# LayerNorm's beta and the attention mask, added by accumulating DMAs instead of GpSimd instructions

## The chip, the cores and the metric

One Trainium2 chip, one of its cores. The metric is the device time of one execution in microseconds (us), from runs on the chip. The engines are TensorE (PE in the profile; PEld is its weight load), VectorE (DVE), ScalarE (ACT), GpSimd (POOL) and SyncE (SP). DMA transfers are issued from the queues of SP, ACT and POOL and share 16 DMA engines.

## What is computed

A trunk of two layers on 256 tokens of 2048 channels, float32. Layer 0 mixes tokens by a bidirectional gated linear attention, layer 1 by a neighbourhood attention of 16 heads on a 4 x 64 grid of tokens; after each mixer comes a gated feed-forward part with a convolution of width 3. Every sub-layer ends in a residual sum and a LayerNorm, four in all:

```python
x = _layer_norm(DEEPNORM_ALPHA * x + m, ln_mix_g[i], ln_mix_b[i])
f = _conv_ffn(x, ffn_w_up[i], ffn_conv_w[i], ffn_conv_b[i], ffn_w_down[i])
x = _layer_norm(DEEPNORM_ALPHA * x + f, ln_ffn_g[i], ln_ffn_b[i])
# _layer_norm: xc * rsqrt(var + eps) * g + b
# attention:   softmax(q k^T + bias), bias = NEG_INF outside the window of 16 columns
```

## The kernel before, in words

All weights (some 405 units of 1 MB, 128 partitions x 2048 floats) are streamed once from HBM. `unit_plan` is the order in which TensorE takes them. SP's queue loads each unit into one of three `raw` buffers (L127). The unit is then split into a rounded high part and a rest: ACT casts `hi` (L131), DVE subtracts to get `lo` (L132), each in four pieces of 128x512, into one of four pairs of buffers (`NS = 4`). A product is the sum of three float32r products, high x high, high x low and low x high (L190). A unit's buffers are free again when TensorE is through with it, and a `raw` buffer when its last `lo` has been made. The same pair of instructions splits every activation that is multiplied; for the output of a LayerNorm it goes from the tile `ln_f` into `xT`.

What is not a large product (gates, attention scores, LayerNorm) stands in a queue `side`; `later` puts a piece in, and `tick`, called between the matrix products, takes it out. Each engine executes its own list in order.

A sub-layer ends in `residual_out`: four blocks of 512 columns for two tiles of 128 tokens (t = 0, 1). The evacuation adds the product to the residual `x_sb` (L360, L362) and takes statistics (L366). The last block runs tile by tile (`apart`), so that the LayerNorm of tile 0 runs beside the products of tile 1. Three of the four LayerNorms are `ln_mid`:

- `head`: DVE aggregates (L282), POOL makes 1/sqrt(var + eps) in two small instructions (L274 `rs_m`, L275 `ln_rs`), DVE normalizes the four blocks of `x_sb` in place (L293).
- `turn`, four times: TensorE transposes four 128x128 pieces (L299), ACT and DVE multiply by gamma and add beta (L307, L309) into `ln_f`, and `emit_split` makes `xT` from it, which the next sub-layer multiplies.
- `resid`: POOL multiplies `x_sb` by gamma (L315) and adds beta (L316), block by block, for the residual that the next sub-layer's first block will read. `gb` holds gamma and beta, repeated on all partitions, 1 MB each (`load_gb`, L344, on POOL's queue).

The last LayerNorm (`ln_last`) writes the output and also uses POOL for one block per tile.

In the attention, each head loads its bias table `bt` (L701, POOL's queue, two buffers), POOL adds the mask to it (L702), and DVE adds `bt` to the scores (L724) when the head's queries and keys are done. In the feed-forward part POOL makes the first product of the convolution (L642) for each of 84 blocks of channels per layer.

Of the kernel before, what the change touches and what calls it, by code (L numbers as in the profile page):

```python
# [10 lines left out]
F32 = mybir.dt.float32  # L11
# [3 lines left out]
ALU = mybir.AluOpType  # L15
AX = mybir.AxisListType

P = 128
D = 2048
# [28 lines left out]
def unit_plan():  # L48
    """The 1 MB weight units in the order in which the tensor engine takes them."""
    plan = []  # L50
    for h in range(HG):
        plan += [("ws", "gla_in", h * 2 + c) for c in range(2)]
        plan += [("ws", "gla_in", 8 + h * 2 + c) for c in range(2)]
        if h == 0:
            plan += [("lr",)]
        plan += [("as", "gla_in", 4 + h, u) for u in range(4)]
        plan += [("as", "gla_in", 8 + h, u) for u in range(4)]
    plan += [("as", "gla_out", nb, u) for nb in range(4) for u in range(4)]
    for layer in range(DEPTH):
        if layer == 1:  # L60
            for g in range(4):
                plan += [("as", "na_in", 8 + g, u) for u in range(4)]
                for h in range(4 * g, 4 * g + 4):
                    plan += [("ws", "na_in", h), ("ws", "na_in", 16 + h)]
            plan += [("as", "na_out", nb, u) for nb in range(4) for u in range(4)]
        for c0, n in THIRDS:
            if c0 == 0:
                plan += [("pairs", f"up{layer}", u) for u in range(4)]
            for c in range(c0 + (2 if c0 == 0 else 0), c0 + n):
                plan += [("ws", f"up{layer}", c), ("ws", f"up{layer}", NCT + c)]  # L70
            plan += [("as", f"down{layer}", nb, u)
                     for nb in range(4) for u in range(c0 // 4, (c0 + n) // 4)]
    return plan
# [3 lines left out]
def kernel(  # L77
# [56 lines left out]
    def pump():  # L134
        while st["split"] < min(n_units, st["done"] + NS):
            j = st["split"]
            while st["load"] < min(n_units, j + NR):
                emit_load(st["load"])
                st["load"] += 1
            r = raws.pop(j)  # L140
            hi = hi_p.tile([P, 2048], F32R, tag="hi", name="hi")
            lo = lo_p.tile([P, 2048], F32R, tag="lo", name="lo")
            if plan[j][0] == "lr":
                # three copies of the columns, for the three terms of the gates' product
                src = r[:, :512].rearrange("p (k m) -> p k m", m=32)
                h4 = hi[:, :KC * 96].rearrange("p (k c m) -> p k c m", c=3, m=32)
                l4 = lo[:, :KC * 96].rearrange("p (k c m) -> p k c m", c=3, m=32)
                for c in range(3):
                    emit_split(src, h4[:, :, c], l4[:, :, c])
            else:  # L150
                for sl in pieces(4):
                    with tc.high_priority(offset=-SPLIT_AFTER):
                        emit_split(r[:, sl], hi[:, sl], lo[:, sl])
            splits[j] = (hi, lo)
            st["split"] = j + 1
            if st["load"] < n_units:
                emit_load(st["load"])
                st["load"] += 1

    def take():  # L160
        """The parts of the next unit."""
        pump()
        j = st["next"]
        st["next"] = j + 1
        return splits.pop(j)
# [7 lines left out]
    def later(fn, delay=1, chain=True):  # L173
        """Emit fn in `delay` ticks: after the item queued before it, or from now on."""
        now = st["tick"]
        due = delay + (max([now] + [d for d, _ in side[-1:]]) if chain else now)
        side.append((due, fn))
        side.sort(key=lambda i: i[0])
# [12 lines left out]

# [1 line left out]
    def ws_part(xs, hi, lo, ps, kcs):  # L193
# [15 lines left out]

# [1 line left out]
    def as_mm(xs, k, kc, hi3, lo3, ps, t, start, stop):  # L211
# [4 lines left out]
    def as_block(xs, n, evac, apart=False, settle=False):  # L216
        """n units (4 chunks of K each) for one block of 512 columns."""
        ps = [ps_mm(), ps_mm()]
# [41 lines left out]

# [1 line left out]
    ident = const.tile([P, P], F32, name="ident")  # L262
# [6 lines left out]

# [1 line left out]
    def rsqrt(dst, src, scale, eps, small):  # L271
        """(src * scale + eps) ** -0.5"""
        m = small.tile([P, 1], F32, tag="rs_m", name="rs_m", bufs=2)
        nc.gpsimd.tensor_scalar(m, src, scale, eps, ALU.mult, ALU.add)  # L274
        nc.gpsimd.tensor_tensor(dst, m, mhalf, ALU.pow)  # L275
# [11 lines left out]
    def ln_mid(pool, xs, t, stats, idx, gb):  # L287
        """LayerNorm between sub-layers: xT for the products, xs for the residual."""
        def head():
# [22 lines left out]
        def resid():  # L312
            for b in range(4):
                sl = slice(b * 512, b * 512 + 512)
                nc.gpsimd.tensor_tensor(xs[:, t, sl], xs[:, t, sl], gb[:, 0, sl], ALU.mult)  # L315
                nc.gpsimd.tensor_tensor(xs[:, t, sl], xs[:, t, sl], gb[:, 1, sl], ALU.add)  # L316

# [5 lines left out]
    def ln_last(pool, xs, t, stats, gb):  # L323
# [15 lines left out]
        later(go, 0)  # L339

    def load_gb(pool, idx):
        gb = pool.tile([P, 2, D], F32, tag="gb", name="gb")
        for i in range(2):
            nc.gpsimd.dma_start(gb[:, i], lnp[idx, i:i + 1, :].broadcast_to([P, D]))  # L344
        return gb

    def residual_out(act_in, first, last, n, idx, begin=None):
        """Four blocks of columns of a product that ends a sub-layer, and the LayerNorm after it."""
        stats = {}
# [23 lines left out]

# [1 line left out]
    scope = {"stack": ExitStack()}  # L375
# [15 lines left out]

    # the first units and x in pieces of K, so that the products start with the first of them
    n_first = NR
# [32 lines left out]

    # the gates as one product over 98 rows: (lr, weights) as (hi, hi), (lo, hi), (hi, lo), and the bias
    lrT = gla.tile([98, T], F32R, name="lrT")
    nc.gpsimd.memset(lrT[96:98, :].bitcast(F32), 1.0)
    # +1 on the rows with weights' high parts, -1 on those with their low parts; 0 and 1  # L430
    sgn = gla.tile([98, 2], F32, name="sgn")
# [24 lines left out]
    def join(pool, dst, ps):  # L456
        """The sum of the two parts of a weights-stationary product."""
        ps4 = ps.rearrange("p (t h n) -> p t h n", t=2, h=2)
# [4 lines left out]
    def gla_head(h):  # L463
# [17 lines left out]
        def gates(z):  # L481
# [12 lines left out]
            else:  # L494
                nc.vector.tensor_tensor_scan(c_[:, ::-1], smask[:, 512:0:-1], la[:, ::-1], 0.0, ALU.mult, ALU.add)
            # [channel, tile of channels, block of 128, half, token]
            c5 = c_.rearrange("p (c b s n) -> p c b s n", c=2, b=2, s=2)
# [9 lines left out]
        def decay(z):  # L507
# [12 lines left out]
            kx[z] = gla.tile([P, 2, P], F32, tag=f"kx{z}", name="kx")  # L520
            # forward: queries of block 1 over chunk 2, keys of block 0 over chunk 1; backward: the mirror
            qb, kb = (1, 0) if z == 0 else (0, 1)
# [7 lines left out]
        def scores():  # L530
            # main[j, jt, it, i]: backward on the diagonal, the crossing blocks beside it
            main, diag = ps_tp(), ps_tp()
# [88 lines left out]

# [1 line left out]
    def ffn(layer):  # L623
# [23 lines left out]
        for part, (c0, n) in enumerate(THIRDS):  # L647
# [16 lines left out]
            if part == 0:  # L664
                # two pairs with the activations stationary, one token tile after the other
                ht = {}
# [20 lines left out]
            if part == 0:  # L687
                scope["gb"] = load_gb(pool, idx)
            residual_out(gT, part == 0, part == len(THIRDS) - 1, n // 4, idx)

# [1 line left out]
    def attention():  # L692
# [3 lines left out]
        def head(h):  # L696
# [4 lines left out]
            nc.gpsimd.dma_start(bt, bias[h])  # L701
            nc.gpsimd.tensor_tensor(bt, bt, mask_sb["m"], ALU.add)  # L702
            v = vt[h // 4]
# [70 lines left out]

# [1 line left out]
    for h in range(HG):  # L776
        gla_head(h)

    def begin_gla_out():
# [5 lines left out]
        nc.gpsimd.dma_start(scope["x"], x.rearrange("(t p) d -> p t d", p=P))  # L785
        scope["gb"] = load_gb(open_pool("ffn0"), 0)

    def begin_na_out():
        scope["gb"] = load_gb(swap_pool("ffn1"), 2)

# [9 lines left out]
def lay_out(a):  # L800
    """The inputs as the kernel reads them: orders, repeats and zero padding only."""
    mats = {"gla_in": a["gla_w_in"][0], "gla_out": a["gla_w_out"][0],
# [67 lines left out]
```

## Time and profile before

| | |
|---|---|
| runs | 2319.03 and 2319.93 us, median 2319.48 |
| profiled execution, first to last instruction (its span) | 2314.5 us |
| PE busy | 2267.8 us, 98% of the span |
| DVE busy | 1576.1 us, 68% |
| ACT busy | 1139.4 us, 49% |
| POOL busy | 314.9 us, 14% |
| DMA queues, share of 16 engines | SP's 49.8%, POOL's 1.8% |
| moved from and to HBM | 186 GB/s over the span |

The page gives the profiled execution by its span alone; the median of the runs is 5.0 us above it, for what lies before the first and behind the last instruction. Busy shares are means over the whole span: an engine with a low share can still hold up the others in a short stretch. A wait names the engine that waited, the line it stood at, and whose result ended the wait. In a timeline, an instruction's time reaches from its start to its end; with a count (x2) it is the time of the whole group, and what stands in brackets is how long the engine was idle before it and for whom.

### The profile page before, as it was taken

How to read it: one execution, taken by the hardware profiler on the slowest of the kernel's cores; microseconds unless marked ns; L12 is line 12 of the kernel's file. 1: busy time of each engine (PE TensorE's matmuls, PEld its weight loads, DVE VectorE, ACT ScalarE, POOL GpSimd, SP SyncE). 2: the span in 40 equal slices, each digit the busy share in tenths (PEclk: the TensorE clock that was granted, in tenths of full speed). 3: DMA queues.
4: the chain of work that ended last, by engine and by line, in shares of the span. 5: the costliest groups of instructions: out<-in, count | busy, mean ns of one | idle time of the engine just before them, and what ended most of it. 6: DMA issues, size and time to landing. Idle time of an engine off the chain costs nothing. (4 is left out here: it accounts for less than half of the span.)

```text
span 2314.5 us, 31264 instructions
## 1 busy us (share of the span) xinstructions
PE 2267.8 (98%) x11728; PEld 1929.9 (83%) x11728; DVE 1576.1 (68%) x2831; ACT 1139.4 (49%) x2307; POOL 314.9 (14%) x333
## 2 busy tenths in 40 slices
PE   8999999899999999999989999989999999999997
PEld 7888887788888888888778888878888888888886
DVE  7666656877557775676686776668775577656775
ACT  6655544554445553444455555445554455444542
POOL 1100002311001110011230111023110011100111
PEclk9999999999999999999999999999999999999999
DMA  7544463555555555555445544545555555555552
GB/s 275 185 164 182 178 260 140 208 196 187 195 187 182 186 193 196 188 184 191 155 178 187 183 174 177 220 144 210 193 187 194 190 191 182 192 190 185 189 191 91
DMA packets 63879, 432.84 MB, mean 187 GB/s; under 512 B 7344, under 2 KB 7344, under 8 KB 12784
## 3 DMA queue, kind: packets, MB, share of 16 engines
q1 hardware_dynamic: 60336, 415.00, 49.8%
q0 software_dynamic: 3104, 15.32, 1.8%
q8 instruction: 92, 1.51, 0.3%
q10 hardware_dynamic: 288, 0.52, 0.1%
q14 instruction: 59, 0.48, 0.1%
HBM read 428.72 MB, written 2.10 MB: 186 GB/s over the span
## 5 line engine op out<-in xcount | busy, mean ns | idle before, releaser
L132 DVE TENSOR_TENSOR lo<-raw,hi 128x512 fp32r<-128x512 f32 x1571 | 1056.3, 701 | 449.7 <-ACT hi L131 448.5
L190 PE MATMUL ps_mm<-xT,hi 128*128 128x512 f32 x3472 | 1231.9, 399 | 6.6 <-ACT hi L131 5.9
L131 ACT CAST hi<-raw 128x512 fp32r<-128x512 f32 x1571 | 884.7, 619 | 615.4 <-PE ps_mm L190 486.9
L190 PE MATMUL ps_mm<-xT,lo 128*128 128x256 f32 x3472 | 976.2, 281 | 0.0
L190 PEld LDWEIGHTS ps_mm<-xT,hi 128*128 128x128 f32 x3472 | 653.2, 188 | 167.0 <-ACT hi L131 5.9
L190 PEld LDWEIGHTS ps_mm<-xT,lo 128*128 128x128 f32 x3472 | 656.9, 189 | 1.5 <-DVE lo L132 0.9
L190 PE MATMUL ps_mm<-hi,gT 128*128 128x512 f32 x1920 | 595.5, 390 | 0.0
L190 PEld LDWEIGHTS ps_mm<-hi,gT 128*128 128x128 f32 x1920 | 360.4, 188 | 74.9
L190 PE MATMUL ps_mm<-lo,gT 128*128 128x512 f32 x960 | 373.5, 389 | 0.0
L642 POOL TENSOR_SCALAR c<-h,cw,cb 128x256 f32<-128x256 f32 x168 | 149.9, 892 | 1171.6 <-DVE h L461 1171.6
L190 PE MATMUL ps_mm<-hi,xT 128*128 128x512 f32 x896 | 286.5, 394 | 0.0
L190 PEld LDWEIGHTS ps_mm<-lo,gT 128*128 128x128 f32 x960 | 180.3, 188 | 36.8
L190 PEld LDWEIGHTS ps_mm<-hi,xT 128*128 128x128 f32 x896 | 170.3, 190 | 35.5 <-DVE xT L132 0.5
L190 PE MATMUL ps_mm<-lo,xT 128*128 128x512 f32 x448 | 177.2, 395 | 7.6 <-DVE lo L132 7.5
L131 ACT CAST gT<-gg 128x256 fp32r<-128x256 f32 x88 | 35.8, 407 | 230.5 <-DVE gg L660 230.5
L643 DVE SCALAR_TENSOR_TENSOR c<-h,cw,c 128x255 f32<-128x255 f32 x168 | 81.2, 484 | 77.9 <-POOL c L642 77.9
L655 ACT ACTIVATE ge<-c 128x256 f32<-128x256 f32 x88 | 36.8, 418 | 156.5 <-DVE c L644 156.5
L190 PEld LDWEIGHTS ps_mm<-lo,xT 128*128 128x128 f32 x448 | 85.5, 191 | 26.3 <-DVE lo L132 9.4
L644 DVE SCALAR_TENSOR_TENSOR c<-h,cw,c 128x255 f32<-128x255 f32 x168 | 80.2, 477 | 0.0
L460 ACT COPY join_t<-ps_mm 128x256 f32<-128x256 f32 x216 | 78.9, 365 | 0.0
L461 DVE TENSOR_TENSOR h<-ps_mm,join_t 128x256 f32<-128x256 f32 x168 | 70.1, 417 | 0.0
L132 DVE TENSOR_TENSOR gT<-gg,gT 128x256 fp32r<-128x256 f32 x88 | 37.4, 425 | 38.7 <-ACT gT L131 38.7
(131 smaller groups left out, 870.1 us busy)
## 6 DMA issues: line engine op xcount, KB each, us to landing
raw<-in_w_dram SPq DMA_DIRECT2D x388, 1024.0 KB, 4.8
gb<-in_lnp_dram POOLq DMA_DIRECT2D x8, 1024.0 KB, 10.4
raw<-in_w_dram SPq DMA_DIRECT2D x16, 256.0 KB, 5.7
bt<-in_bias_dram POOLq DMA_DIRECT2D x16, 192.0 KB, 2.9
xr<-in_xt_dram SPq DMA_DIRECT2D x8, 256.0 KB, 5.6
x_sb<-in_x_dram POOLq DMA_DIRECT2D x1, 2048.0 KB, 10.3
out_dram<-x_sb SPq DMA_DIRECT2D x6, 256.0 KB, 2.3
gu<-in_gup_dram POOLq DMA_DIRECT2D x4, 196.0 KB, 3.3
```

Source lines behind the costliest of these rows:

```text
L131: nc.scalar.copy(hi, src)
L132: nc.vector.tensor_tensor(lo, src, hi.bitcast(F32), ALU.subtract)
L190: nc.tensor.matmul(o, l, r, start=start, stop=stop)
L460: nc.scalar.copy(tmp, ps4[:, :, 1])
L461: nc.vector.tensor_tensor(dst.rearrange("p (t n) -> p t n", t=2), ps4[:, :, 0], tmp, ALU.add)
L642: nc.gpsimd.tensor_scalar(c, hh, w_[:, 1:2], cb[:, ch:ch + 1], ALU.mult, ALU.add)
L643: nc.vector.scalar_tensor_tensor(c[:, 1:], hh[:, :T - 1], w_[:, 0:1], c[:, 1:], ALU.mult, ALU.add)
L644: nc.vector.scalar_tensor_tensor(c[:, :T - 1], hh[:, 1:], w_[:, 2:3], c[:, :T - 1], ALU.mult, ALU.add)
L655: nc.scalar.activation(ge, c, AF.Gelu)
```

## The change

In `resid` the four POOL additions of beta per token tile are replaced by one DMA, issued on POOL's queue, that reads beta from HBM, repeated on 128 partitions, and adds it to the 1 MB of `x_sb` in SBUF (`accum_op=ALU.add`). `gb` shrinks to gamma alone (`load_g`) for the three LayerNorms between sub-layers; the last one keeps both. In the attention the POOL addition of the mask to `bt` is replaced by a DMA from the mask's tile in SBUF that adds to `bt`. The rest of the difference removes comments.

```diff
@@ ln_mid, resid
             for b in range(4):
                 sl = slice(b * 512, b * 512 + 512)
-                nc.gpsimd.tensor_tensor(xs[:, t, sl], xs[:, t, sl], gb[:, 0, sl], ALU.mult)
-                nc.gpsimd.tensor_tensor(xs[:, t, sl], xs[:, t, sl], gb[:, 1, sl], ALU.add)
+                nc.gpsimd.tensor_tensor(xs[:, t, sl], xs[:, t, sl], gb[:, sl], ALU.mult)
+            nc.gpsimd.dma_start(xs[:, t], lnp[idx, 1:2, :].broadcast_to([P, D]), accum_op=ALU.add)
...
+    def load_g(pool, idx):
+        g = pool.tile([P, D], F32, tag="gb", name="g")
+        nc.gpsimd.dma_start(g, lnp[idx, 0:1, :].broadcast_to([P, D]))
+        return g
+
...
@@ ffn
-                scope["gb"] = load_gb(pool, idx)
+                scope["gb"] = (load_gb if idx == 2 * DEPTH - 1 else load_g)(pool, idx)
...
@@ attention, head
             nc.gpsimd.dma_start(bt, bias[h])
-            nc.gpsimd.tensor_tensor(bt, bt, mask_sb["m"], ALU.add)
+            nc.gpsimd.dma_start(bt, mask_sb["m"], accum_op=ALU.add)
...
@@ begin_gla_out, begin_na_out
-        scope["gb"] = load_gb(open_pool("ffn0"), 0)
+        scope["gb"] = load_g(open_pool("ffn0"), 0)
...
-        scope["gb"] = load_gb(swap_pool("ffn1"), 2)
+        scope["gb"] = load_g(swap_pool("ffn1"), 2)
```

The lists of PE, DVE, ACT and SP are the same in both kernels, row for row, except that lines below 340 have other numbers (L360 is L365 in the changed kernel, L642 is L647). Only POOL's list differs. At the first LayerNorm between sub-layers, before (`rs_m` and `ln_rs` belong to a tile's `head`, the rows on `x_sb` to its `resid`):

```order
L274 TENSOR_SCALAR rs_m<-ln_mv 128x1
L275 TENSOR_TENSOR ln_rs<-rs_m,mhalf 128x1
L315 TENSOR_TENSOR x_sb<-x_sb,gb 128x512 x2
L316 TENSOR_TENSOR x_sb<-x_sb,gb 128x512 x2
L315 TENSOR_TENSOR x_sb<-x_sb,gb 128x512
L316 TENSOR_TENSOR x_sb<-x_sb,gb 128x512
L315 TENSOR_TENSOR x_sb<-x_sb,gb 128x512
L316 TENSOR_TENSOR x_sb<-x_sb,gb 128x512
L274 TENSOR_SCALAR rs_m<-ln_mv 128x1
```

and the same place in the changed kernel:

```order
L274 TENSOR_SCALAR rs_m<-ln_mv 128x1
L275 TENSOR_TENSOR ln_rs<-rs_m,mhalf 128x1
L315 TENSOR_TENSOR x_sb<-x_sb,g 128x512 x4
L316 DMA x_sb<-in_lnp_dram 128x2048
L274 TENSOR_SCALAR rs_m<-ln_mv 128x1
L275 TENSOR_TENSOR ln_rs<-rs_m,mhalf 128x1
L315 TENSOR_TENSOR x_sb<-x_sb,g 128x512 x4
L316 DMA x_sb<-in_lnp_dram 128x2048
```

Between the heads of tile 0 and tile 1 POOL now has four multiplications and the issue of one DMA, where it had eight instructions on 128x512. The first rows of the attention on POOL in the changed kernel, each `L707` being the transfer that adds the mask:

```order
L772 DMA bmask_sb<-in_bmask_dram 128x384
L706 DMA bt<-in_bias_dram 128x384 x2
L707 DMA bt<-bmask_sb 128x384 x2
L706 DMA bt<-in_bias_dram 128x384
L707 DMA bt<-bmask_sb 128x384
L706 DMA bt<-in_bias_dram 128x384
```

The order is that of before, with a DMA in the place of each addition on POOL.

## Rows read from the trace of the kernel before

**Rows 1.** The page: busy time, share of the span and instructions of each engine.
```profile
PE 2267.8 (98%) x11728; PEld 1929.9 (83%) x11728; DVE 1576.1 (68%) x2831; ACT 1139.4 (49%) x2307; POOL 314.9 (14%) x333
```

**Rows 2.** Waits of PE: line, releaser, us in total, times, longest.
```profile
PE ps_tp L299 <- DVE x_sb L293: 16.5, 3, 6.0
PE ps_mm L190 <- DVE lo L132: 7.5, 3, 2.9
```

**Rows 3.** Stretches: length, busy PE, PEld, DVE, ACT, POOL, clock, DMA share, GB/s.
```profile
384.00:426.00 42.00, 32.68 (x147) 26.45 (x146) 40.06 (x57) 22.17 (x45) 30.47 (x22) 0.92 0.28 101
425.00:440.00 15.00, 15.00 (x81) 12.84 (x80) 10.66 (x19) 9.58 (x18) 0.00 (x0) 1.00 0.95 382
1172.00:1175.00 3.00, 2.96 (x7) 2.38 (x8) 3.00 (x4) 0.98 (x2) 2.74 (x2) 0.50 0.00 0
1180.00:1470.00 290.00, 290.00 (x1631) 252.16 (x1630) 206.87 (x390) 157.16 (x358) 28.98 (x30) 1.00 0.52 187
```

**Rows 4.** Timeline of POOL, first LayerNorm: start, us, line, operation, idle before.
```profile
392.87 3.44 POOL L316 TENSOR_TENSOR x_sb<-x_sb,gb 128x512 f32<-128x512 f32 x2
396.28 1.74 POOL L315 TENSOR_TENSOR x_sb<-x_sb,gb 128x512 f32<-128x512 f32 x1
...
406.93 0.49 POOL L274 TENSOR_SCALAR rs_m<-ln_mv 128x1 f32<-128x1 f32 x1 [3.81 <-DVE ln_mv L282]
...
412.65 3.44 POOL L316 TENSOR_TENSOR x_sb<-x_sb,gb 128x512 f32<-128x512 f32 x2
```

**Rows 5.** Timeline of DVE, the same LayerNorm.
```profile
393.39 3.48 DVE L132 TENSOR_TENSOR xT<-ln_f,xT 128x512 fp32r<-128x512 f32 x2
396.79 1.78 DVE L132 TENSOR_TENSOR lo<-raw,hi 128x512 fp32r<-128x512 f32 x1
...
400.83 1.14 DVE L132 TENSOR_TENSOR lo<-raw,hi 128x512 fp32r<-128x512 f32 x1
401.89 2.37 DVE L132 TENSOR_TENSOR xT<-ln_f,xT 128x512 fp32r<-128x512 f32 x2
...
404.79 0.68 DVE L132 TENSOR_TENSOR lo<-raw,hi 128x512 fp32r<-128x512 f32 x1
...
416.56 1.77 DVE L132 TENSOR_TENSOR xT<-ln_f,xT 128x512 fp32r<-128x512 f32 x1
...
418.58 1.45 DVE L132 TENSOR_TENSOR lo<-raw,hi 128x512 fp32r<-128x512 f32 x1
...
420.60 1.11 DVE L132 TENSOR_TENSOR lo<-raw,hi 128x512 fp32r<-128x512 f32 x1
```

**Rows 6.** Timeline of DVE, second LayerNorm.
```profile
1152.70 1.78 DVE L132 TENSOR_TENSOR lo<-raw,hi 128x512 fp32r<-128x512 f32 x1
...
1158.07 0.25 DVE L282 BATCH_NORM_AGGREGATE ln_mv<-ln_st 128x2 f32<-128x24 f32 x1
...
1166.86 3.47 DVE L132 TENSOR_TENSOR xT<-ln_f,xT 128x512 fp32r<-128x512 f32 x2
...
1170.57 1.42 DVE L132 TENSOR_TENSOR lo<-raw,hi 128x512 fp32r<-128x512 f32 x1
```

**Rows 7.** Timeline of POOL, second LayerNorm, where tile 1 begins.
```profile
1156.95 2.32 POOL L316 TENSOR_TENSOR x_sb<-x_sb,gb 128x512 f32<-128x512 f32 x1
1159.36 0.51 POOL L274 TENSOR_SCALAR rs_m<-ln_mv 128x1 f32<-128x1 f32 x1
```

**Rows 8.** One line of the program, L344 (1 MB of `gb`): issue on POOL, time to landing.
```profile
L344 POOL DMA_DIRECT2D gb<-in_lnp_dram x8: 528/559/612, 311.6 to 1577.6; - x8
...
DMA to landing us min/median/max: 5.4/10.4/18.9
```

**Rows 9.** Lines L701 (192 KB of `bt`) and L702 (mask): waits of POOL.
```profile
POOL bt L701 <- DVE s L724: 197.1, 14, 31.2
...
POOL bt L702 <- DMA bt<-in_bias_dram: 39.8, 15, 5.0
```

**Rows 10.** Timeline of ACT behind the first LayerNorm.
```profile
435.38 1.67 ACT L131 CAST hi<-raw 128x512 fp32r<-128x512 f32 x3 [2.25 <-DMA raw<-in_w_dram]
```

## The prediction

> **What bounds the kernel now.** I read the page's busy times first. TensorE is busy for 98% of the span [rows 1]: the kernel is bound by its matrix products, and an edit that leaves every engine's list but POOL's as it was can only pay where PE stands still. So I read next what PE waits for. Apart from the start and the end of the program, nearly all of it is two waits, each met three times, once per LayerNorm between sub-layers: PE's transposes wait for the normalized rows of tile 1, 16.5 us in all, and a product waits for a `lo`, 7.5 us in all [rows 2]. The third view is the stretch of one such LayerNorm: in 42 us PE is busy for 32.7, DVE for 40.1 and POOL for 30.5 [rows 3]. There DVE is the bound, and POOL, elsewhere a bystander, is at work all the time. The fourth view, the two timelines side by side, shows why DVE is late. A `lo` piece of 128x512 takes 0.68 us at 404.79, while POOL is idle; between 393 and 403, while POOL multiplies and adds on `x_sb`, the same instruction takes 1.78 and 1.14 us, and two `xT` pieces 3.48 us [rows 4, 5]. A DVE subtraction that reads two SBUF tiles is slowed while POOL works on SBUF; that is a fact of these rows, whatever its cause.
>
> Elsewhere POOL's work costs nothing. In the attention PE is busy for 290.0 of 290 us [rows 3], although POOL's sixteen mask additions lie in it.
>
> **The additions of beta.** Three LayerNorms, two tiles, four additions each: 24 POOL instructions of some 1.7 us go (3.44 us for two [rows 4]). None of them is on the path by itself; what counts is how soon DVE is rid of POOL.
>
> First LayerNorm, tile 0. POOL makes two multiplications, then two additions from 392.87 to 396.31, then a multiplication of 1.74 us [rows 4]. In the changed order the third and fourth multiplication take the place of those two additions, so POOL falls silent at about 396.4, and not only after four more instructions of some 1.7 us, near 403. DVE is as before until 396.79. Behind that, `lo` goes from 1.78 to 0.68 us (gain 1.10), two more `lo` from about 1.14 to 0.68 (the one shown at 400.83 and its twin: 0.92), the `xT` pair from 2.37 to at most 1.36 (1.01) [rows 5]. That is 3.0 us. DVE's list then holds the last evacuation of tile 1 and its statistics, so `rs_m` of tile 1, the normalization and PE's restart come 3.0 us earlier.
>
> First LayerNorm, tile 1. POOL's first two additions start at 412.65 and take 3.44 us [rows 4]; the last two multiplications stand there instead, and POOL is silent from about 416.1. Then `xT` goes from 1.77 to 0.68, `lo` from 1.45 and from 1.11 to 0.68: 2.3 us [rows 5]. The `lo` wait that this shortens lasts at most 2.9 us [rows 2], so all of it counts. Sum 5.3 us. The third LayerNorm repeats the first instruction by instruction, so 5.3 again.
>
> Second LayerNorm. Tile 0: `lo` at 1152.70 goes from 1.78 to 0.68, 1.1 us; and `rs_m`, ready for at 1158.32 when DVE has aggregated, starts only at 1159.36 because POOL is in an addition: 1.0 us [rows 6, 7]. Tile 1: of the `xT` pair of 3.47 us the second piece becomes free (1.0 to 1.1), and the `lo` of 1.42 becomes 0.68 (0.7): 1.8 us [rows 6]. Behind that wait PE works for 3 us at a granted clock of 0.50, 1.2 GHz, having stood still for up to 2.9 us [rows 2, 3]. At full clock the same work takes 1.5 us. With a gap of about 1 us the clock may stay up; I take half, 0.8 us. Sum 4.7 us.
>
> **Total:** 5.3 + 5.3 + 4.7 = 15.3 us. PE's two waits hold 24.0 us, so there is room for it.
>
> The rows show contention by single instructions. The Trainium skill gives a rule for it ("SBUF — State Buffer", section "Who interferes with whom"): a DVE instruction with two SBUF inputs shares a read port with GpSimd, and the one that issues second blocks until the first has ended. By that rule each addition taken out could free DVE for the whole of it, 8 x 1.7 = 13.6 us per LayerNorm, which would close PE's waits entirely: 2292 us, where the rows give 2304. The trace agrees only in part: `xT` pieces do last as long as a POOL instruction (3.48 us for two), but between them DVE reads PSUM and `lo` pieces get through in 1.14 us. I count by the rows.
>
> **The DMAs that add beta.** Six, 1 MB each, issued on POOL behind the fourth multiplication; against them three loads of beta go. Issuing one of that size takes POOL at most 612 ns [rows 8]. Behind it in POOL's list stands `rs_m` of tile 1, for which POOL waits 3.81 us even now and, with 6.7 us less work, over 7 us [rows 4]. Nobody waits for the result soon: the next to touch that part of `x_sb` is the first block of the next sub-layer's residual, at least 28 weight units later, at some 5.6 us each (2267.8 us over 405 units) about 157 us. No row shows an accumulating transfer. Its nearest row is `gb`, the same bytes without the reading of the destination: 5.4 us at the fastest, 10.4 at the median, 18.9 at the slowest [rows 8]. If the reading doubles the slowest, 37.8 us is the upper end. I take 10.4; at 10.4 it costs nothing.
>
> By the Trainium skill ("DMA: Bandwidth & Descriptors", "Anatomy of one DMA") a transfer from POOL's queue takes about 2.0 us plus its bytes at 436 GB/s, an estimate of 4.4 us for 1 MB; by it the sum stays the same.
>
> **The DMAs that add the mask.** Sixteen POOL additions go, sixteen transfers of 192 KB come. `bt` has two buffers, so a table is loaded as soon as the scores two heads earlier have been made, and is read two heads later: 2 x 290 / 16 = 36 us. Load and wait take about 2.7 us (39.8 us in 15 waits) [rows 9]. Even a transfer of 18.9 us fits. While POOL now waits for a load, only `bt` rows stand behind it, and POOL idles there for 197.1 us already [rows 9]. DVE gets freer, PE is full: gain 0, and 0 lost.
>
> **Smaller terms.** The first `load_g` moves 1 MB instead of 2 before the first LayerNorm: nothing waits for it. The convolution's POOL work and the last LayerNorm keep their instructions. All 0.
>
> **How it could go otherwise.**
>
> *Rival 1, no gain:* DVE, rid of POOL, waits for ACT's casts and `ln_f` instead, since the two alternate in the same list. For it: ACT is busy for 22 of the 42 us [rows 3], and its casts are tied to DVE's pieces. Against it: DVE is busy for 40.1 of 42, so it hardly ever waits for ACT now. If two thirds or more of the 15.3 us go this way: 2314 to 2320 us. Chance 0.14.
>
> *Rival 2, DVE gets back all the time that the additions take:* eight of some 1.7 us are 13.6 us per LayerNorm [rows 4], more than PE waits there, so the waits of 24.0 us vanish, and with them some 3 us of half clock (twice what I counted in the second LayerNorm): about 2292 us. For it: two `xT` pieces take 3.48 us, two POOL additions 3.44 [rows 4, 5]. Against it: the 1.14 us pieces, and the multiplications still run at the start of each tile. Chance 0.06. This is what the rule of "SBUF — State Buffer" in the Trainium skill would make of the change.
>
> *Rival 3, slower:* the transfer of tile 1 is slow and sits in front of the weights. Its place is the stretch from 425 to 440, where the three `raw` buffers are refilled and the DMA engines are 95% busy at 382 GB/s [rows 3]. There ACT already waits 2.25 us for a weight, ending at 435.38 [rows 10]. That unit is needed only after 2.7 us of a product begun at about 433 and two units of 5.6 us, at 447; its split ends at about 438, so 9 us are to spare. The transfer starts at about 417, some 6 us before the weights move again, so it decides from about 15 us on. Against it: it has only 8 rows of 8 KB per engine, and takes the place of a beta load. At 20 us the gain is used up; at 37.8, with the weights held up all the while, each LayerNorm loses 23 us: 2304 + 69 = 2373. Chance 0.09, of which 0.04 lie more than 2% above before.
>
> **The numbers.** My forecast has 0.70; the remaining 0.01 is for what I don't see. From the median of 2319.5 (the profiled span of 2314.5 lies 5.0 below it, for what is outside the first and last instruction; the sum is a difference inside the span) I get 2319.5 - 15.3 = 2304. Its own range is 2298 to 2311: the low end adds the clock in all three LayerNorms, the high end halves the gain. The range for 8 in 10 reaches on to most of rival 1: 2297 to 2319. About 2%, 46 us, is what a measurement of this kernel can tell from no change. No case but rival 3 reaches past that, and PE's waits are too short for a gain of 46 us: faster 0.01, same 0.95, slower 0.04.
>
> **What would show it.** In the changed profile: L316 no longer among POOL's busy lines; `lo` and `xT` near 0.68 us in the second half of each tile; PE's wait for the normalized rows from 16.5 to about 8.5 us and that for `lo` from 7.5 to about 1; the waits of the attention as they are. The forecast is wrong if the `xT` pieces keep their 1.7 us, if DVE's gaps for ACT grow by as much as its pieces shrink, or if ACT's waits for `raw` behind a LayerNorm exceed 9 us.

## The result and the profile after

The changed kernel takes 2304.28 us (median of two runs, 2301.29 and 2307.28) against 2319.48 before: ratio 0.9938, 95% interval 0.9919 to 0.9956. Timed again beside the experiments it took 2304.37 us (five runs), ratio 0.9936, interval 0.9923 to 0.9949. The forecast was 2304. It is a gain of 15 us, 0.6%, and the intervals keep it clear of no change: the 2% that the prediction named as the limit of such a measurement was too coarse.

The page of the changed kernel, busy time and share of each engine, answers to [rows 1]. The profiled span is 2299.5 us, 15.0 less.

```profile
PE 2261.2 (98%) x11728; PEld 1925.5 (84%) x11728; DVE 1548.9 (67%) x2831; ACT 1141.3 (50%) x2307; POOL 272.4 (12%) x312
```

POOL has 42.5 us less to do, and the kernel is 15 us shorter. Where the time was gained shows in PE's waits, the same view as [rows 2]:

```profile
PE ps_tp L299 <- DVE x_sb L293: 8.7, 3, 3.0
...
PE ps_mm L190 <- DVE lo L132: 3.7, 3, 1.8
PE ps_tp L299 <- DVE ln_f L309: 3.4, 4, 1.0
PE ps_mm L190 <- DVE xT L132: 1.6, 2, 1.2
PE ps_tp L681 <- ACT ht L675: 1.1, 1, 1.1
```

The wait for the normalized rows of tile 1 has nearly halved, from 16.5 to 8.7 us, and the wait for a `lo` has halved, from 7.5 to 3.7.

The first LayerNorm shows the mechanism. POOL's timeline first, to be laid beside [rows 4]: four multiplications, then one issue of a DMA, then nothing until `rs_m` of tile 1 is due.

```profile
388.52 8.07 POOL L315 TENSOR_TENSOR x_sb<-x_sb,g 128x512 f32<-128x512 f32 x4 [1.92 <-PE ps_tp L299]
396.90 0.95 POOL L316 DMA_DIRECT2D x_sb<-in_lnp_dram  x1 [0.31 <-POOL x_sb L315]
404.10 0.48 POOL L274 TENSOR_SCALAR rs_m<-ln_mv 128x1 f32<-128x1 f32 x1 [6.25 <-DVE ln_mv L282]
```

DVE's timeline in the same stretch, against [rows 5]:

```profile
393.66 3.48 DVE L132 TENSOR_TENSOR xT<-ln_f,xT 128x512 fp32r<-128x512 f32 x2
397.06 0.68 DVE L132 TENSOR_TENSOR lo<-raw,hi 128x512 fp32r<-128x512 f32 x1
...
398.31 0.68 DVE L132 TENSOR_TENSOR lo<-raw,hi 128x512 fp32r<-128x512 f32 x1
...
399.54 0.68 DVE L132 TENSOR_TENSOR lo<-raw,hi 128x512 fp32r<-128x512 f32 x1
400.14 1.29 DVE L132 TENSOR_TENSOR xT<-ln_f,xT 128x512 fp32r<-128x512 f32 x2
...
413.79 0.68 DVE L132 TENSOR_TENSOR xT<-ln_f,xT 128x512 fp32r<-128x512 f32 x1
...
416.05 0.68 DVE L132 TENSOR_TENSOR lo<-raw,hi 128x512 fp32r<-128x512 f32 x1
```

Up to 397 the two kernels are alike (the changed one 0.27 us later), down to the 3.48 us of the `xT` pair: POOL is still multiplying. From then on the pieces of tile 0 that took 1.78, 1.13, 1.14 or 2.37 us take 0.68 (or 1.29 for two), and the order of the list is the same. These pieces alone are 3.09 us shorter, and `rs_m` of tile 1 stands 18.34 us behind that of tile 0, where it was 21.44: 3.10 us. In tile 1 it is the same: the pieces stay slow beside the multiplications, and from 413.79 on, when POOL has ended them, they take 0.68.

What sets the length of a slow piece shows when both engines' starts are laid side by side. In the kernel before, the second and third `lo` of tile 0 and the POOL instructions beside them:

```profile
399.13 1.13 DVE L132 TENSOR_TENSOR lo<-raw,hi 128x512 fp32r<-128x512 f32 x1
400.83 1.14 DVE L132 TENSOR_TENSOR lo<-raw,hi 128x512 fp32r<-128x512 f32 x1
...
398.10 1.62 POOL L316 TENSOR_TENSOR x_sb<-x_sb,gb 128x512 f32<-128x512 f32 x1
399.67 1.75 POOL L315 TENSOR_TENSOR x_sb<-x_sb,gb 128x512 f32<-128x512 f32 x1
401.50 1.61 POOL L316 TENSOR_TENSOR x_sb<-x_sb,gb 128x512 f32<-128x512 f32 x1
```

The two `lo` start 1.70 us apart, and so, on average, do the POOL instructions (398.10 to 401.50 for two). In the changed kernel, with POOL silent, the same two start 1.23 us apart (398.31 and 399.54). The `xT` pair and the `lo` behind it (393.39 to 396.79 for two, [rows 5]) go at 1.70 us as well. In these rows one DVE subtraction with two SBUF inputs gets through for each POOL instruction.

Two lines of the program, the accumulating transfers of beta (L316) and of the mask (L707): the issue on POOL (ns, least, median, most) and the time to landing.

```profile
L316 POOL DMA_DIRECT2D x_sb<-in_lnp_dram x6: 912/922/952, 396.9 to 1558.5; - x6
...
DMA to landing us min/median/max: 7.6/8.5/9.1
...
L707 POOL DMA_DIRECT2D bt<-bmask_sb x16: 844/854/905, 1176.1 to 1434.7; - x16
...
DMA to landing us min/median/max: 2.9/3.1/8.3
```

No row of any engine names either of them as a releaser: nobody waits for them. In the attention (1180 to 1470, columns as in [rows 3]) PE is as full as before, and DVE is busy for 13 us less, which gains nothing:

```profile
1180.00:1470.00 290.00, 290.00 (x1631) 252.29 (x1630) 194.13 (x387) 155.38 (x355) 21.53 (x31) 1.00 0.59 196
```

### The profile page after: what moved, and what is told of

Read it like the earlier page. It is cut to its first block, busy times and chain, and to the rows that moved or that the text cites. A ratio compares the mean times of both kernels' runs of the same rounds, so it can differ in the third digit from the quotient of the medians.

```text
span 2299.5 us, 31248 instructions
## 1 busy us (share of the span) xinstructions
PE 2261.2 (98%) x11728; PEld 1925.5 (84%) x11728; DVE 1548.9 (67%) x2831; ACT 1141.3 (50%) x2307; POOL 272.4 (12%) x312
## 5 line engine op out<-in xcount | busy, mean ns | idle before, releaser
L132 DVE TENSOR_TENSOR lo<-raw,hi 128x512 fp32r<-128x512 f32 x1571 | 1042.3, 692 | 456.2 <-ACT hi L131 453.9
L647 POOL TENSOR_SCALAR c<-h,cw,cb 128x256 f32<-128x256 f32 x168 | 149.8, 892 | 1179.6 <-DVE h L466 1179.6
```

The lines of the kernel that those rows point to most:

```text
L132: nc.vector.tensor_tensor(lo, src, hi.bitcast(F32), ALU.subtract)
L647: nc.gpsimd.tensor_scalar(c, hh, w_[:, 1:2], cb[:, ch:ch + 1], ALU.mult, ALU.add)
```

## The experiments

**One half at a time.** The first kernel has beta by DMA and the mask by POOL, the second the mask by DMA and beta by POOL:

```diff
# first: from the changed kernel
-            nc.gpsimd.dma_start(bt, mask_sb["m"], accum_op=ALU.add)
+            nc.gpsimd.tensor_tensor(bt, bt, mask_sb["m"], ALU.add)
# second: from the kernel before
-            nc.gpsimd.tensor_tensor(bt, bt, mask_sb["m"], ALU.add)
+            nc.gpsimd.dma_start(bt, mask_sb["m"], accum_op=ALU.add)
```

> Only beta by accumulating DMAs; the mask stays an addition on GpSimd. Theory A (DVE is rid of GpSimd's additions in the three LayerNorms, nothing else counts): all of the gain is here, 2304 us, 15 below before; PE's wait for the normalized rows near 8.7 us, that for lo near 3.7 as in the changed kernel. Rival M (the mask's part gives or costs something, too): between 2304 and 2319, or below 2302 if the mask's DMAs cost time.

> Only the mask by accumulating DMAs; beta stays on GpSimd. Theory A: no change, 2318 to 2321 us, PE without a wait in the attention, DVE there some 10 us less busy. Rival M: 2310 or below, or above 2322.

Beta alone: 2305.26 us, ratio 0.9934 (0.9921 to 0.9946). The mask alone: 2318.27 us, ratio 0.9996 (0.9987 to 1.0006). The gain is beta's, and the mask's sixteen transfers neither give nor cost anything that these runs can tell from nothing. With beta alone PE waits for 8.7 us for the rows, as expected, and for 2.8 for a `lo`, where I expected 3.7; below it is seen that this wait differs with the clock. With the mask alone, PE's waits are about as before:

```profile
PE ps_tp L299 <- DVE x_sb L293: 16.5, 3, 6.0
PE ps_mm L190 <- DVE lo L132: 8.4, 3, 3.2
```

**No beta at all.** The line with L316 is deleted, so the residual lacks beta.

```diff
-            nc.gpsimd.dma_start(xs[:, t], lnp[idx, 1:2, :].broadcast_to([P, D]), accum_op=ALU.add)
```

> The changed kernel without the six DMAs that add beta to the residual (that addition is left out; everything else is computed). Theory A with hidden transfers: as the changed kernel, 2303 to 2305 us. Rival D (the transfers cost time behind a LayerNorm, where weights are late): faster than the changed kernel by what they cost, 2300 or less, and ACT's waits for weights (20.9 us in the changed kernel) fall.

2301.97 us, ratio 0.9925 (0.9913 to 0.9938), against 0.9934 (0.9921 to 0.9946) for beta alone, timed beside it on the same chip. This lies between what I expected of hidden transfers and of rival D. The intervals overlap: six transfers of 1 MB may cost 2 us (0.0009 of the time; the medians differ by 3.3), and that isn't told from nothing here. ACT's waits for weights are 18.0 us without them,

```profile
ACT hi L131 <- DMA raw<-in_w_dram: 18.0, 14, 3.7
```

where the changed kernel has 20.9; PE has no wait of its own for a transfer in either. So no cost of the transfers is shown, and a few us stay possible.

**POOL work put back, reading and writing: two that tested nothing.** One POOL instruction per multiplication was to be put back, an addition that reads SBUF or memsets that only write it, beta still coming by DMA. The tile of gamma gets a second half that nobody reads, for these instructions to write.

```diff
-                nc.gpsimd.tensor_tensor(xs[:, t, sl], xs[:, t, sl], gb[:, sl], ALU.mult)
+                nc.gpsimd.tensor_tensor(xs[:, t, sl], xs[:, t, sl], gb[:, 0, sl], ALU.mult)
+                nc.gpsimd.tensor_tensor(gb[:, 1, sl], gb[:, 0, sl], gb[:, 0, sl], ALU.add)
...
# the other kernel, in the same place
+                for _ in range(2):
+                    nc.gpsimd.memset(gb[:, 1, sl], 0.0)
```

> The changed kernel with one GpSimd addition of 128x512 put back behind each multiplication; it reads gamma twice and writes a buffer that nobody reads, so beta still comes by DMA. Theory A: the gain is lost, 2318 to 2321 us, PE's two waits back at 16 and 7 us, xT pieces at 1.7 us. Rival C (what counted was the dependency on x_sb, or beta's loads): stays at 2304.

> The changed kernel with two GpSimd memsets of 128x512 behind each multiplication, into a buffer that nobody reads: GpSimd is busy, but it only writes SBUF. If DVE's slowness comes from the reading of SBUF that it shares with GpSimd: stays near 2304 us, with lo and xT near 0.68 us while memsets run; at most 1 us per LayerNorm where a memset stands in front of rs_m. Rival (any work of GpSimd on SBUF slows DVE, in proportion to its time): up to 2319.

2304.98 and 2304.93 us, both as the changed kernel. But POOL's timeline shows the additions 60 us ahead of the LayerNorm, since they depend on nothing but gamma and were scheduled as soon as it had landed:

```profile
329.79 7.37 POOL L316 TENSOR_TENSOR g<-g 128x512 f32<-128x512 f32 x6
```

The memsets, too, ran ahead of the LayerNorm that they were meant for. So these two runs do not test contention in the LayerNorm. I repeated them with the instructions pinned behind the four multiplications.

```diff
+            for b in range(4):
+                sl = slice(b * 512, b * 512 + 512)
+                tc.keep_in_program_order(nc.gpsimd.tensor_tensor(gb[:, 1, sl], gb[:, 0, sl], gb[:, 0, sl], ALU.add))
# the other kernel, in the same place
+                for _ in range(2):
+                    tc.keep_in_program_order(nc.gpsimd.memset(gb[:, 1, sl], 0.0))
```

> The changed kernel with four GpSimd additions of 128x512 pinned behind the four multiplications of each tile, so that they run where beta's additions ran; they read gamma and write an unused buffer, and beta's DMA follows them. Theory A (DVE's subtractions are slowed by GpSimd instructions that read SBUF): the gain is lost, 2317 to 2321 us, lo at 1.1 to 1.8 us and the second xT pair near 2.4 us, PE's waits for the normalized rows back at about 16 us. Rival C (the dependency on x_sb or beta's own data made the difference): stays at 2304.

> The same with eight memsets of 128x512 in place of the four additions, some 4 us of GpSimd per tile that only writes SBUF. If only GpSimd's reads slow DVE: near 2304 us, at most 1 us per LayerNorm above, lo at 0.68 us while memsets run. Rival (any GpSimd work on SBUF slows DVE): lo and xT there at 1.0 us or more, 2309 to 2314 us.

With additions that read: 2312.13 us, ratio 0.9973 (0.9963 to 0.9982). With memsets: 2300.65 us, ratio 0.9918 (0.9905 to 0.9932). The timelines of POOL and DVE in the first LayerNorm, additions first:

```profile
396.33 5.83 POOL L318 TENSOR_TENSOR g<-g 128x512 f32<-128x512 f32 x4
...
396.84 1.52 DVE L132 TENSOR_TENSOR lo<-raw,hi 128x512 fp32r<-128x512 f32 x1
...
398.93 0.89 DVE L132 TENSOR_TENSOR lo<-raw,hi 128x512 fp32r<-128x512 f32 x1
...
400.37 0.88 DVE L132 TENSOR_TENSOR lo<-raw,hi 128x512 fp32r<-128x512 f32 x1
...
401.18 2.12 DVE L132 TENSOR_TENSOR xT<-ln_f,xT 128x512 fp32r<-128x512 f32 x2
```

and memsets:

```profile
397.59 4.01 POOL L319 MEMSET g<- 128x512 f32 x7
...
397.01 0.68 DVE L132 TENSOR_TENSOR lo<-raw,hi 128x512 fp32r<-128x512 f32 x1
...
398.25 0.68 DVE L132 TENSOR_TENSOR lo<-raw,hi 128x512 fp32r<-128x512 f32 x1
...
400.10 1.28 DVE L132 TENSOR_TENSOR xT<-ln_f,xT 128x512 fp32r<-128x512 f32 x2
```

Additions that have nothing to do with `x_sb` or beta slow DVE's pieces again; memsets in the same microseconds don't slow one of them. From the start of `rs_m` of tile 0 to PE's restart behind the `lo` wait, the first LayerNorm takes 36.28 us before and 31.03 in the changed kernel; it takes 34.57 with the additions and 31.01 with the memsets (third LayerNorm: 36.26, 30.98, 34.55 and 31.00). Rival C falls: it was not the dependency.

The size was off: I expected the whole gain to be lost, and half was (7.6 of 15 us between the medians of before and this kernel remain). The added instruction is shorter than an addition of beta, 5.83 us for four (1.46 each) against 3.44 for two (1.72) [rows 4], and each of DVE's pieces is shorter by about as much: 1.52 where it was 1.78, 0.89 and 0.88 where it was 1.13 and 1.14, 2.12 where it was 2.37. The second and third `lo` start 1.44 us apart. It is again one subtraction for each POOL instruction.

(In the memset kernel a few DVE pieces of the second LayerNorm stand in another order; in the first and third they stand as in the changed kernel. Its 3.7 us below the changed kernel are inside overlapping intervals.)

**The multiplications moved, too.** If POOL's reads beside a LayerNorm are the cost, they can all be put where DVE has time. In the first of two kernels nothing comes by DMA: `resid` of the first and third LayerNorm stays on POOL and is emitted block by block, one for every second weight unit of the next product. In the second, the changed kernel's multiplications are moved like that in all three (in the attention with loads of 512 columns of gamma at a time), and the DMA follows each tile's last block.

```diff
# both kernels
-        later(resid, 0)
...
+            held_resid.extend((lambda b=b: resid(b)) for b in range(4))
...
                 ws_one(xT, lambda ps: evac(i, ps))
+                if i % 2 and held_resid:
+                    held_resid.pop(0)()
...
# the second kernel
+            tc.keep_in_program_order(nc.gpsimd.tensor_tensor(xs[:, t, sl], xs[:, t, sl], gb[:, sl], ALU.mult))
```

> The kernel before with all of resid on GpSimd, but in the first and third LayerNorm emitted later, one block of 512 columns for every second weight unit of the next product; no accumulating DMA. Theory A: DVE is rid of multiplications and additions in two of three LayerNorms, 8 to 9 us each: about 2303 us. Rival (the moved work holds up DVE or the convolution there as much): 2312 to 2325.

> The changed kernel with the multiplications by gamma emitted later in all three LayerNorms (in the attention block by block with small loads of gamma), then the accumulating DMAs: no GpSimd work beside the LayerNorms. Theory A: 8 to 9 us in each of three, about 2294 us, faster than both kernels. Rival (PE's waits have another floor): 2300 to 2305.

> The changed kernel, as a measure beside the others: 2304 us by theory A; 15 us below the kernel before.

Without any DMA, two LayerNorms only: 2296.55 us, ratio 0.9896 (0.9881 to 0.9911). With the DMA, all three: 2286.09 us, ratio 0.9854 (0.9840 to 0.9867). Both are faster than the kernel before and than the changed one (the intervals do not meet), and the first shows that the accumulating DMA is not what makes the time; to get POOL out of the way is. Both gave more than I expected (23.7 and 34.2 us against 16 and 25). PE's waits in the last kernel:

```profile
PE ps_mm L190 <- DVE xT L132: 1.9, 2, 1.6
PE ps_tp L299 <- DVE ln_f L309: 1.7, 3, 0.6
PE ps_tp L299 <- DVE x_sb L293: 1.1, 3, 0.4
```

and its first LayerNorm, columns as in [rows 3]:

```profile
384.00:426.00 42.00, 41.01 (x204) 33.91 (x203) 36.83 (x72) 29.69 (x60) 1.78 (x4) 1.00 0.46 170
```

PE works through it, 41.0 of 42 us, and the granted clock is 1.00 where it was 0.92, as it is in all three LayerNorms of the two kernels. That is the part that I had not counted: 0.08 of 42 us is an estimate of at most 3.4 us per LayerNorm.

The moved work is not free on DVE. The instructions of the convolution that read SBUF twice, in the moved kernel (432 to 520) and in the kernel before (445 to 533):

```profile
L671 DVE SCALAR_TENSOR_TENSOR c<-h,cw,c 128x255 f32<-128x255 f32 x16 | 15.9, 991 | 7.4 <-POOL c L670 7.4
```

```profile
L643 DVE SCALAR_TENSOR_TENSOR c<-h,cw,c 128x255 f32<-128x255 f32 x17 | 8.2, 484 | 7.8 <-POOL c L642 7.8
```

The 991 ns are a mean of two kinds. Eight of the sixteen take 0.48 us as before; the eight that have a multiplication beside them take 1.50, three times as long:

```profile
443.79 0.48 DVE L671 SCALAR_TENSOR_TENSOR c<-h,cw,c 128x255 f32<-128x255 f32 x1 [0.47 <-POOL c L670]
448.41 1.50 DVE L671 SCALAR_TENSOR_TENSOR c<-h,cw,c 128x255 f32<-128x255 f32 x1 [0.47 <-POOL c L670]
...
448.35 1.29 POOL L317 TENSOR_TENSOR x_sb<-x_sb,g 128x512 f32<-128x512 f32 x1
```

PE is busy for 88.0 of 88 us in both stretches, so the 1.0 us that each of the eight loses is hidden.

## Why the prediction was right, point by point

**The bound and the place** held: DVE's pieces gain 5.25, 3.78 and 5.28 us in the three LayerNorms, 14.3 in all, where the forecast without the clock had 14.5; the half with the mask is worth nothing that can be measured. That the total also came to 15 is in part luck: what is left over, below, nearly cancels.

**The first and third LayerNorm, 5.3 us each.** From the start of `rs_m` of tile 0 to PE's restart behind the `lo` wait it was 36.28 us before (385.49 to 421.77 in the first), and it is 31.03 after (385.76 to 416.79): 5.25. In the third, 36.26 and 30.98: 5.28. The pieces went to the 0.68 us that I had taken from one row.

**The second, 4.7 us.** By the same measure 30.64 and 26.86, 3.8 us, where I had 3.9 without the clock.

**The clock** was the term that I had least hold on, and its size was a guess. In the second LayerNorm I took half of 1.5 us. There the gap before the `lo` shrank to 1.09 us, and up to the next LayerNorm the kernel gains 5.3 us (the `rs_m` of the second and of the third are 397.95 us apart before, 392.61 after): all of the 1.5. The first LayerNorm of this execution gives it back. Behind its second gap of 1.77 us, which I had expected to close, the clock falls for a while, as the stretch behind PE's restart shows, in the changed kernel and in the kernel before:

```profile
416.80:430.00 13.20, 13.20 (x52) 10.78 (x53) 8.09 (x14) 7.78 (x16) 0.00 (x0) 0.87 0.99 330
```

```profile
421.80:435.00 13.20, 13.20 (x63) 11.09 (x64) 9.93 (x15) 7.70 (x15) 2.21 (x3) 1.00 0.91 359
```

A mean of 0.87 over 13.2 us is 3.4 us at 0.50, 1.2 GHz, so 1.7 us of work lost, and up to the next LayerNorm only 3.6 of the 5.25 us are left (755.92 and 752.29 us between the first two `rs_m`).

It is the first LayerNorm by chance. In the kernel before, PE had stood still for 6.03 us before the transposes, and the clock fell there, before the `lo` gap; in the changed kernel that gap is 3.01 us long, and in its first LayerNorm the clock stays up behind it. First the stretch behind the transposes' gap, before and changed:

```profile
408.70:413.70 5.00, 5.00 (x18) 4.52 (x19) 4.81 (x10) 2.34 (x6) 3.81 (x3) 0.50 0.46 157
405.90:410.00 4.10, 3.77 (x24) 2.98 (x25) 4.10 (x8) 2.26 (x5) 3.38 (x3) 1.00 0.50 138
```

Then another execution of the changed kernel (`e8_changed_again`), behind the `lo` gap of its first and of its third LayerNorm:

```profile
417.70:430.00 12.30, 12.24 (x55) 9.99 (x55) 7.19 (x13) 6.87 (x14) 0.00 (x0) 1.00 1.02 363
1559.40:1572.60 13.20, 13.15 (x52) 10.72 (x53) 9.11 (x15) 8.43 (x16) 0.00 (x0) 0.87 1.02 366
```

There the first LayerNorm has the slow stretch behind the transposes' gap (a clock of 0.65 from 406.80 to 411.50), and the third has it behind the `lo` gap (1.00 from 1548.50 to 1552.50, behind the transposes' gap). In front of the `lo` gap it costs nothing, since DVE sets the time (31.01 us to PE's restart in that execution, against 31.03); behind it, it costs 1.7 us. In both executions one LayerNorm of the three loses the 1.7 us, and not the same one. So the clock as a whole gave about nothing (1.5 gained, 1.7 lost), where the forecast had 0.8.

From the third LayerNorm to the end the gain is 6.3 us (775.14 and 768.84): 5.28 up to PE's restart, 1.62 from there to the last LayerNorm (719.63 and 718.01 us), and 0.60 lost behind that. In the stretch of the 1.62 PE takes 175 matmuls in 30 us where before it took 172 (1621.64 to 1651.64 and 1635.62 to 1665.62), with no gap and the clock at 1.00 in both; why, stays open. With 0.3 us of later start, 3.6 + 5.3 + 6.3 - 0.3 is the 15 us of the span.

**PE's waits** came out as 8.7 us for the rows (about 8.5 forecast) and 3.7 for `lo` (about 1 forecast). The second was mis-sized: PE, restarted sooner and for part of the way at the higher clock, comes to that `lo` sooner as well (9.14 us behind its restart in the first LayerNorm, where it took 10.81), so a gap stays though the `lo` is ready earlier. The time did not suffer, because DVE sets it there.

**The price of the transfers.** I took 10.4 us for 1 MB, between 5.4 and 37.8; it is 8.5. The issue on POOL is 0.92 us, more than the 0.61 of the nearest row; with 6.25 us of idle time behind it that costs nothing. By the Trainium skill ("DMA: Bandwidth & Descriptors", "Anatomy of one DMA") 1 MB would land in 4.4 us, an estimate from its fit; the accumulating transfers take about twice that, and the measurement decides. Whether the adding is what makes them slower is not shown: the plain loads of 1 MB had a median of 10.4 us [rows 8].

**The rivals.** No gain (rival 1) fell: DVE did not wait for ACT instead; in the first LayerNorm, between 388 and 420 us, its one wait is of 0.73 us, for `ln_rs`. The slow transfer (rival 3) fell with 8.5 us against the 15 from which it would have decided. Rival 2 is wrong for this change, but what it lives on is shown: the rule of the Trainium skill ("SBUF — State Buffer", "Who interferes with whom") says that DVE with two SBUF inputs contends with GpSimd instructions that read SBUF, and not with those that only write. The pinned additions and memsets agree with both halves: 1.52 and 0.89 us against 0.68. The prediction set the blocking aside because of the pieces of 1.14 us; the rows agree with it, too. Such a piece comes when part of the POOL instruction is over, because DVE read PSUM before it (399.13 in an addition that runs from 398.10 to 399.72), and only the rest is waited for. What was wrong in rival 2 is the price: taking a POOL instruction away does not give DVE its 1.7 us, but what DVE lost on it, 0.47 us where reads of PSUM stand between the pieces (1.70 to 1.23) and about 1.1 where the piece follows directly (1.78 to 0.68).

## What to carry to other kernels

An engine that is 14% busy can hold up the one that is 98% busy, if in a short stretch its work slows the engine on which that one waits: read the same instruction's duration with and without the neighbour at work before costing the neighbour at nothing, and single instructions rather than the mean of a group. An accumulating DMA is a way to take an addition from GpSimd where its result is not needed soon; moving the work to a stretch where DVE has time gave more, even without any DMA. And where a gap of PE is shortened, look at the granted clock behind it, and in more than one execution.

## What the runs showed of the hardware

- An accumulating DMA of 1 MB from HBM onto SBUF lands in 7.6 to 9.1 us, one of 192 KB from SBUF onto SBUF in 3.1 (median); the issue holds POOL for 0.84 to 0.95 us, against 0.56 (median) for a plain load of 1 MB or of 192 KB.
- Beside DVE in the LayerNorm, a GpSimd addition of 128x512 takes 1.46 us when both its inputs are the same tile, and 1.72 on `x_sb` and beta; a memset of that size 0.57 us. Only the additions slow DVE: one subtraction with two SBUF inputs gets through for each of them (1.44 and 1.70 us from start to start, 1.23 with GpSimd silent).
- PE's clock fell to 0.50 behind a gap of 1.77 us in one LayerNorm of the changed kernel, where it had stayed at 1.00 behind one of 3.01 us just before; behind one of 2.27 us at the same place in the kernel before, where it had already fallen behind one of 6.03 us, it did not. Which of the two gaps it falls behind differs between executions of the same kernel. The length of the last gap alone does not tell it.
